# A hybrid decoder layer: attention's first q and k tiles, gate tiles and the evacuation of G put elsewhere in a planned order

## The chip, the cores and the metric

The kernel runs on one core of a Trainium2 chip. The metric is the time of one execution in microseconds (us), as the device measures it; the median of several runs counts. The engines are TensorE (PE), VectorE (DVE), ScalarE (ACT), GpSimd (POOL) and the DMA-issuing queue of SyncE (SP). Each runs its own instructions strictly in the order in which the program holds them.

## The reference

One layer over a sequence of 512 tokens, width 2048. The input is normalised and projected; half of the projection's columns feed 16 heads of dilated attention, half feed 16 heads of a recurrence (RWKV-7), and each half has a gate.

```python
h = rms_norm(x, norm_g[l])
proj = jnp.matmul(h, w_in[l]).astype(jnp.float32)
q, k, v, z_att, u_shift, z_rwkv = jnp.split(proj, splits, axis=-1)
att = dilated_mixture_attention(q, k, v, pos) * jax.nn.silu(z_att)
rwk = rwkv7_time_mix(u_shift, z_rwkv, ...)
x = x + jnp.matmul(jnp.concatenate([att, rwk], axis=-1), w_out[l])
return rms_norm(x, final_g)

# in dilated_mixture_attention: q, k rotated by position, three dilations
q = apply_rope(q.reshape(B, S, N_ATT_HEADS, HEAD_DIM), pos) * (HEAD_DIM ** -0.5)
k = apply_rope(k.reshape(B, S, N_ATT_HEADS, HEAD_DIM), pos)

# in rwkv7_time_mix, and one step of its recurrence
k = k * (1.0 + (a - 1.0) * k_a)
sa = jnp.einsum('bhij,bhj->bhi', state, a_t)
state = state * w_t + sa[..., None] * b_t + v_t[..., None] * k_t
y = jnp.einsum('bhij,bhj->bhi', state, r_t)
y = y_normed + bonus
return y * g * jax.nn.silu(z)
```

## The kernel before

**Tiles and fillers.** The projection is made in tiles of 128 columns for all 512 tokens. A tile takes 48 matmuls of 128x512: 16 slices of the contraction, three products each (weights and activations are split in a high and a low part, `whi`, `wlo`, `hh`, `hl`). The results are `mm_lora`, `mm_k`, `mm_r`, `mm_v` (the recurrence), `mm_z` (gates), `mm_gl`, `mm_qk` (attention's q and k); the attention's values come in three blocks `mv`. The weights arrive by SP's queue in tiles `raw_*` of 512 KB; ACT writes `whi` from them and DVE `wlo`. These matmuls are the fillers: they depend on little, and PE runs through them without a stop.

**The small work between them.** Python generators ("sides") hold the dependent steps: `pre`, `subst`, `build`, `scan`, `att`, `gate_g` and others. A side issues some instructions and then yields with an estimate and the tiles it needs next. After every filler matmul `step` calls `pump`, which lets go on those sides whose data a simple cost model of the engines holds to be ready. So the order of every engine's program is fixed when the kernel is built, and it is a guess: where a tile comes later than the model held, the in-order engine waits.

**The recurrent part** (to about 650 us). The 16 heads go as 8 pairs p, in chunks of 64 tokens. For each pair the tiles k, r, v are projected; `pre` makes the decay and rate (`pw`, `pa`, `wc`, `W`), the matrix `pM` of the triangular system and the bonus `pb`. `subst` solves the system in 62 steps that alternate between POOL's and DVE's tiles `XT`, `Xtmp`. Two merging steps follow (`zpb`), then `build`: two matmul groups `zf` whose results are copied to `L` by ACT and DVE, and four tiles G (`gp`, 128x512 each) which DVE multiplies by a mask into `X`. `scan` then runs over the chunks (`Y`, with `A`, `yc`), and `pF`, `pQ` prepare the next pair. Before all that `load_x` squares x, sums it into `acc`, and `rms` has PE sum `acc` over partitions (`pr`, `prb`); every projected result is scaled by `rstd` when it is evacuated, so the first evacuations (`first_evac`) wait for it.

**The attention** (650 to 965 us). 16 tiles `mm_qk`, four for each group g of four heads (two for q, two for k), are rotated (`rope_evac`, POOL and DVE, tiles `m`), and `assemble` moves the rotated rows by SP DMAs in pieces of 32 rows into `qa`, `ka`, from which ACT and DVE make high and low parts (`q`, `kd`, `kl`). `att` makes scores `s`, transposes `pt`, outputs `po` for each pair of heads. `att_consts` loads the rotary constants and masks into buffers `Lb`, `xt_b` of the recurrent part when that is done. Under the second half of the scores run the gate tiles z8 to z15 and, per pair, the recurrence's gate `pg`, whose weights `gw` are loaded by `gate_g`. The output projection (`raw_o`, `mo`, `mh`, `mt`) ends the program.

**What orders tiles** is the list at the program's end: `EARLY` says how many z tiles stand ahead of each pair's k, r, v, and `add_call` puts planner calls such as `until` between tiles.

Of the kernel before, what the change touches and what calls it, by code (L numbers as in the profile page):

```python
# [20 lines left out]
P = 128  # L21
# [115 lines left out]
def hymba_kernel(ctx: ExitStack, tc: tile.TileContext, xT, x, wa, wb, wo, pv, w2a2, g2, fg,  # L137
# [51 lines left out]
    bonesr = cp.tile([P, P], F32R, name="bonesr")  # L189
    hw0 = cp.tile([P, 16], F32, name="hw0")  # L190
    omu = cp.tile([P, 27], F32, name="omu")
    V.tensor_scalar(omu, pvt[:, 0:27], -1.0, 1.0, ALU.mult, ALU.add)
# [8 lines left out]
    def prologue():  # L201
# [7 lines left out]
        def squares():  # L209
            for k in range(KT):  # L210
                S.activation(xs[k], xs[k], AF.Square)
                if k == 1:
                    V.tensor_tensor(acc, xs[0], xs[1], ALU.add)
                elif k:
                    V.tensor_tensor(acc, acc, xs[k], ALU.add)
                if k % 2:
                    yield 0.0, S
            yield 2.0, acc
            yield from rms(acc)
# [34 lines left out]
    def later():  # L254
        bones = k2([P, P], "bones")
        Q.dma_start(bones, cst[:, 576:704])
        Q.dma_start(bmt, bmask)
        yield 1.59, bones
        V.tensor_copy(bonesr, bones)
        V.tensor_scalar(hw0, pvt[:, PV["w0"]:PV["w0"] + 16], 0.5, None, ALU.mult)  # L260
        for i in range(2):
            G.memset(xt_b[i], 0.0)
            G.tensor_copy(Lb[i][H[i], :, H[i]], ident[H[i], H[i]][:, None, :].to_broadcast([64, NCH, C]))
            yield 0.5, G
# [95 lines left out]
    def pump():  # L360
# [19 lines left out]
        mark[0] = model.clock  # L380

    def first_evac(f, a):
        while not normed:
            yield 0.675
        f(a)
        yield 0.6

# [53 lines left out]
    def run_main():  # L441
        for kind, name, fn in items:
            if kind == "c":
                fn()
            elif kind == "a":
                acc_ps = pm.tile([P, T], F32, tag="mm", name=f"mm_{name}")
                for kc in range(2):
                    hi, lo = feed.get()
                    for kk in range(8):
# [7 lines left out]
                        step()  # L457
                if normed:
                    after(2, lambda f=fn, a=acc_ps: f(a))
                else:  # L460
                    start(first_evac(fn, acc_ps))
# [156 lines left out]
    def pre(p, r, k, v):  # L618
# [82 lines left out]
        start(subst(p, Mp, rn2), 0.06, Mp, rn2, rank=-1)  # L701
        V.tensor_scalar(a, a, -1.0, col("k_a", p), ALU.add, ALU.mult)
        V.scalar_tensor_tensor(k, a, 1.0, k, ALU.add, ALU.mult)
# [109 lines left out]
    def build(p):  # L813
        while p not in state or p not in merged:
            yield 0.5
        st = state[p]
        X, L, FT, xt = (st[n] for n in ("X", "L", "FT", "xt"))
        for q in range(2):
            z = ps(f"zf{p}{q}", (P, 4, P))
            for c4 in range(4):  # L820
                for h in range(2):
                    TE.matmul(z[H[1 - h], c4, :], xt[H[h], 4 * q + c4, :], FT[H[h], 4 * q + c4, :], start=True, stop=True)
            for h in range(2):
                evac(L[h][H[1 - h], 4 * q:4 * q + 4, :], z[H[1 - h]])
            yield 0.3
        for q in range(2):
            for h in range(2):
                gp = ps(f"gp{p}{q}{h}", (P, 4, P))
                for c4 in range(4):
                    TE.matmul(gp[:, c4, :], L[h][:, 4 * q + c4, :], X[h][:, 4 * q + c4, :], start=True, stop=True)  # L830
                V.tensor_tensor(X[h][:, 4 * q:4 * q + 4, :], gp, gmask[h][:, None, :].to_broadcast([P, 4, P]), ALU.mult)
                yield 0.3
        built.add(p)
# [60 lines left out]
    rp, am = [], []  # L894

    def att_consts():
        for i in range(2):
            c_ = Lb[0].rearrange("p c t -> p (c t)")[:, i * T:(i + 1) * T]
            Q.dma_start(c_, rope[i])
            G.tensor_tensor(c_, c_, rstd, ALU.mult)  # L900
            rp.append(c_)
        for i, (o_, n_) in enumerate(((0, 384), (384, 384), (768, 512))):
# [14 lines left out]
    def v_evac(b, acc_ps):  # L917
# [7 lines left out]
        if b == 2:  # L925
            gtok = k1([P, 4, 32], "gtok")
            for t in range(4):
                S.activation(gtok[:, t, :], acc_ps[t][:, n:VB], AF.Copy, scale=rtok[:, t:t + 1])
            start(gl32(gtok), 1.023)

# [35 lines left out]

    pairs = {}

    def assemble(g, j, rot):
        raws = []  # L970
        for pr_ in range(2):
            for h in range(2):
                raw_ = k2([P, T], f"{'qk'[j]}a_{g}{pr_}{h}")
# [5 lines left out]
                raws.append(raw_)  # L979
            yield 5.1  # L980
        yield 0.225, *raws
        for pr_ in range(2):
            tl_ = pairs.setdefault(2 * g + pr_, {})
            if j == 0:
                q_ = k4([P, 2, T], f"q_{g}{pr_}", F32R)
                for h in range(2):
                    raw_ = raws[2 * pr_ + h]
                    S.activation(q_[:, h, :], raw_, AF.Copy)
                    r = H[1 - h]
                    V.tensor_tensor(q_[r, h, :], raw_[r], q_[r, h, :].bitcast(F32), ALU.subtract)  # L990
                tl_["q"] = q_
            else:
                for h in range(2):
                    raw_ = raws[2 * pr_ + h]
                    kd = k2([P, T], f"kd_{g}{pr_}{h}", F32R)
                    klo = k2([P, T], f"kl_{g}{pr_}{h}", F32R)
                    S.activation(kd, raw_, AF.Copy)
                    V.tensor_tensor(klo, raw_, kd.bitcast(F32), ALU.subtract)
                    tl_["k", h] = kd
                    tl_["kl", h] = klo  # L1000
            yield 2.874
        if j == 1:
            start(att(g))

# [4 lines left out]
    def att(g):  # L1009
        units = [(2 * g + pr_, t) for pr_ in range(2) for t in range(4)]  # L1010
        po, ssb_, pts = {}, {}, {}
        for u in range(len(units) + 2):
            if u < len(units):
                pair, t = units[u]
                tl_ = pairs[pair]
                n = max(256, 128 * (t + 1))
                nv = 128 * (t + 1)
                tsl = slice(t * P, (t + 1) * P)
                for h in range(2):
# [8 lines left out]
                    S.activation(ss[:, 0:nv], ss[:, 0:nv], AF.Exp, bias=nm, scale=-1.0, accum_out=den)  # L1028
                    ssb_[u, h] = (ss, den)
            if u >= 2:  # L1030
                pair, t = units[u - 2]
# [194 lines left out]
    add_aa((0, 9), ("lora", "k0"), (lora_evac, lambda a: rkv_evac(0, "k", 8, a)))  # L1226
    NZ, EARLY = 8, {2: 1, 3: 1, 4: 1, 5: 1, 6: 1, 7: 1}
    zs = iter(range(NZ))
# [7 lines left out]
    for p in range(NP):  # L1236
# [6 lines left out]
        add_a(1 + 16 + p, f"v{p}", lambda a, p=p: rkv_evac(p, "v", 16 + p, a))  # L1243
    add_z(NZ)
    add_a(41, "gl128", gl128_evac)
    add_call(lambda: until(lambda: NP - 1 in half))
    add_call(v_alloc)
# [5 lines left out]
    add_call(att_consts)  # L1253
    for g in range(4):
        for i in range(4):
            add_a(25 + 4 * g + i, f"qk{g}{i}", lambda a, g=g, i=i: rope_evac(g, i, a))
    for p in range(NP):
        add_call(lambda p=p: start(gate_g(p), 0.21))
        if p == NP - 1:
            add_call(lambda: pre_mix())  # L1260
        add_a(50 + p, f"z{8 + p}", lambda a, p=p: gate(8 + p, a))
    def pre_mix():
        drain()
# [128 lines left out]
```

## Time and profile before

| | |
|---|---|
| median of 3 runs | 1171.65 us (1171.32 to 1172.88) |
| profiled execution | 1172.79 us |
| its span in the trace | 1170.7 us |
| mean granted PE clock | 0.99 of 2.4 GHz |
| PE busy | 1133.5 us, 6878 instructions |
| DVE busy | 760.2 us |
| ACT busy | 544.0 us |
| POOL busy | 333.9 us |

The busy time of PE is a union of instructions that overlap; a filler of 128x512 lasts 0.39 us in the trace, and the next begins 0.23 us after it. Where PE is at the lower clock, or stands still, the table by stretches shows it. "Waited for" in the wait lists is the time that an engine stood idle before an instruction and the instruction that released it last.

### The profile page before, as it was taken

The numbers are of one execution on the slowest core, as the hardware profiler recorded it, in microseconds if no ns is written. First come the engines' busy times: TensorE is split into PE (matmuls) and PEld (weight loads), VectorE is DVE, ScalarE is ACT, GpSimd is POOL, SyncE is SP. The second block draws the span as 40 slices with busy tenths as digits, with TensorE's granted clock in tenths as the row PEclk, the third lists the DMA queues.
The fourth block names the chain that finished last, engine by engine and source line by source line (L and its number), as shares of the span: only waits on it lengthen the run. The fifth ranks groups of instructions, "written<-read, shape, count | busy, mean of one in ns | idle before, by whom it ended". The sixth has DMA issues, their size and how long they took to land. (4 is left out here: it accounts for less than half of the span.)

```text
span 1170.7 us, 19091 instructions
## 1 busy us (share of the span) xinstructions
PE 1133.5 (97%) x6878; PEld 943.2 (81%) x6878; DVE 760.2 (65%) x1521; ACT 544.0 (46%) x1209; POOL 333.9 (29%) x586
## 2 busy tenths in 40 slices
PE   7999999999999989999999999999999999999997
PEld 5777877788777878789999888888787877888897
DVE  6758867878887788787645555666666656243252
ACT  6444544655546464674533423455454444232233
POOL 1005882643865075644600121110000000011020
PEclk9999999999999989999999999999999999999999
DMA  7334342334242423333342545434344336444333
GB/s 263 101 92 127 105 128 73 95 104 117 78 123 89 115 83 95 91 97 105 88 109 77 162 128 154 123 118 140 109 139 138 117 118 211 126 126 132 103 127 144
DMA packets 89870, 139.62 MB, mean 119 GB/s; under 512 B 37936, under 2 KB 47664, under 8 KB 89776
## 3 DMA queue, kind: packets, MB, share of 16 engines
q1 hardware_dynamic: 89344, 137.83, 39.3%
q8 instruction: 54, 0.88, 0.3%
q10 hardware_dynamic: 432, 0.58, 0.1%
q14 instruction: 40, 0.33, 0.1%
HBM read 114.44 MB, written 14.75 MB: 110 GB/s over the span
## 5 line engine op out<-in xcount | busy, mean ns | idle before, releaser
L88 POOL TENSOR_TENSOR Xtmp<-XT,Mp 128x248 f32<-128x248 f32 (+30 forms) x248 | 128.9, 520 | 182.6 <-DVE XT L88 165.2
L88 POOL TENSOR_TENSOR XT<-XT,Xtmp 128x248 f32<-128x248 f32 (+30 forms) x248 | 142.2, 573 | 21.4 <-DVE XT L88 2.5
L88 DVE TENSOR_TENSOR wlo<-raw_o,whi 128x512 fp32r<-128x512 f32 x64 | 48.1, 792 | 87.5 <-ACT whi L88 87.5
L121 PE MATMUL mm_z<-hl,whi 128*128 128x512 f32 x256 | 103.3, 403 | 0.0
L121 PE MATMUL mm_z<-hh,wlo 128*128 128x512 f32 x256 | 103.0, 402 | 0.0
L121 PE MATMUL mm_z<-hh,whi 128*128 128x512 f32 x256 | 102.8, 402 | 0.0
L121 PE MATMUL mm_qk<-hh,whi 128*128 128x512 f32 x256 | 101.1, 395 | 0.8 <-ACT gtok L88 0.8
L121 PE MATMUL mm_qk<-hh,wlo 128*128 128x512 f32 x256 | 100.8, 394 | 0.0
L121 PE MATMUL mm_qk<-hl,whi 128*128 128x512 f32 x256 | 100.3, 392 | 0.0
L88 POOL TENSOR_TENSOR y<-y,fg 128x512 f32<-128x512 f32 (+1 forms) x16 | 19.3, 1240 | 254.7 <-ACT mo L88 235.9
L88 ACT ACTIVATE ss<-ss,nm 128x128 f32<-128x128 f32 (+3 forms) x64 | 35.5, 556 | 100.8 <-DVE nm L88 100.8
L88 ACT ACTIVATE whi<-raw_o 128x512 fp32r<-128x512 f32 x64 | 36.8, 623 | 95.5 <-PE mo L121 70.4
L88 POOL TENSOR_TENSOR m<-m,m 128x512 f32<-128x512 f32 x16 | 22.6, 1431 | 187.9 <-DVE m L88 144.8
L121 PE MATMUL mo<-whi,mh 128*128 128x512 f32 x192 | 74.7, 389 | 0.0
L121 PE MATMUL mo<-wlo,mh 128*128 128x512 f32 x192 | 74.7, 389 | 0.0
L121 PE MATMUL mo<-whi,ml 128*128 128x512 f32 x192 | 74.7, 389 | 0.0
L88 DVE TENSOR_TENSOR wlo<-raw_qk,whi 128x512 fp32r<-128x512 f32 x64 | 49.6, 795 | 33.1 <-ACT whi L88 29.0
L88 DVE TENSOR_TENSOR wlo<-raw_v,whi 128x352 fp32r<-128x352 f32 (+1 forms) x80 | 50.0, 655 | 26.9 <-ACT whi L88 26.4
L121 PE MATMUL mv<-whi,hh 128*128 128x352 f32 x192 | 63.6, 331 | 1.3 <-DVE vt L88 0.9
L121 PE MATMUL mv<-whi,hl 128*128 128x352 f32 x192 | 62.9, 328 | 0.0
L121 PE MATMUL mv<-wlo,hh 128*128 128x352 f32 x192 | 62.3, 325 | 0.0
L88 DVE TENSOR_TENSOR wlo<-raw_z,whi 128x512 fp32r<-128x512 f32 x64 | 47.9, 766 | 18.8 <-ACT whi L88 18.4
(300 smaller groups left out, 3016.7 us busy)
## 6 DMA issues: line engine op xcount, KB each, us to landing
raw_z<-in_wa_dram SPq DMA_DIRECT2D x32, 512.0 KB
raw_qk<-in_wa_dram SPq DMA_DIRECT2D x32, 512.0 KB
raw_o<-in_wo_dram SPq DMA_DIRECT2D x32, 512.0 KB
raw_v<-in_wb_dram SPq DMA_DIRECT2D x24, 352.0 KB
raw_r<-in_wa_dram SPq DMA_DIRECT2D x16, 512.0 KB
raw_v<-in_wa_dram SPq DMA_DIRECT2D x16, 512.0 KB
raw_k<-in_wa_dram SPq DMA_DIRECT2D x15, 512.0 KB
xk<-in_xT_dram SPq DMA_DIRECT2D x16, 256.0 KB
```

The lines of the kernel that those rows point to most:

```text
L88: return fn(o, *args, **kw)
L121: return fn(o, lhs, rhs, **kw)
```

## The change

- `pr`, the matmul that sums the squares, is asked for later (7.0 instead of 2.0 in the model's time), and first evacuations take turns.
- `(a - 1) k_a` moves from DVE to ACT, with a new constant `nka`.
- `build` waits for both copies of L before `gp`, and each G tile is evacuated in two halves, a copy on ACT and a masked multiply on DVE.
- The four q and k tiles of group 0 (`qk00` to `qk03`) stand ahead of the value blocks, and so do the rotary constants, now loaded to buffers of their own and multiplied on POOL there (`rope_consts`); `att_consts` copies them to `Lb`.
- `assemble` goes by pair of heads, waits for the last value block's evacuation and until the pair two before is scored, and `att` starts when the first pair's k is made.
- `gate_g` of a pair starts one gate tile earlier.
- `EARLY` puts all eight z tiles ahead of or among the pairs.

```diff
-            yield 2.0, acc
+            yield 7.0, acc
...
-        while not normed:
-            yield 0.675
+        turns.append(a)
+        return in_turn(f, a)
+
+    def in_turn(f, a):
+        while not normed or turns[0] is not a:
+            yield 0.3
         f(a)
+        turns.pop(0)
         yield 0.6
...
-        V.tensor_scalar(a, a, -1.0, col("k_a", p), ALU.add, ALU.mult)
+        S.activation(a, a, AF.Identity, bias=nka[:, p:p + 1], scale=col("k_a", p))
...
             yield 0.3
+        yield 0.1, L[0], L[1]
         for q in range(2):
             for h in range(2):
                 gp = ps(f"gp{p}{q}{h}", (P, 4, P))
+                o, qs = H[1 - h], slice(4 * q, 4 * q + 4)
                 for c4 in range(4):
                     TE.matmul(gp[:, c4, :], L[h][:, 4 * q + c4, :], X[h][:, 4 * q + c4, :], start=True, stop=True)
-                V.tensor_tensor(X[h][:, 4 * q:4 * q + 4, :], gp, gmask[h][:, None, :].to_broadcast([P, 4, P]), ALU.mult)
-                yield 0.3
+                S.copy(X[h][:, qs, H[h]], gp[:, :, H[h]])
+                V.tensor_tensor(X[h][:, qs, o], gp[:, :, o], gmask[h][:, None, o].to_broadcast([P, 4, C]), ALU.mult)
+                yield 0.1
...
+    def rope_consts():
+        for i in range(2):
+            c_ = k2([P, T], f"rope{i}")
+            Q.dma_start(c_, rope[i])
+            G.tensor_tensor(c_, c_, rstd, ALU.mult)
+            rp.append(c_)
+
     def att_consts():
         for i in range(2):
             c_ = Lb[0].rearrange("p c t -> p (c t)")[:, i * T:(i + 1) * T]
-            Q.dma_start(c_, rope[i])
-            G.tensor_tensor(c_, c_, rstd, ALU.mult)
-            rp.append(c_)
+            S.copy(c_, rp[i])
+            rp[i] = c_
...
     def assemble(g, j, rot):
-        raws = []
+        while not glt.get("v"):
+            yield 0.5
         for pr_ in range(2):
+            pair = 2 * g + pr_
+            while pair >= 2 and pair - 2 not in scored:
+                yield 0.5
+            raws = []
...
-    NZ, EARLY = 8, {2: 1, 3: 1, 4: 1, 5: 1, 6: 1, 7: 1}
+    NZ, EARLY = 8, {2: 1, 3: 1, 4: 2, 5: 1, 6: 1, 7: 2}
...
     add_a(41, "gl128", gl128_evac)
+    add_call(rope_consts)
+    add_qk(0)
...
-    for g in range(4):
-        for i in range(4):
-            add_a(25 + 4 * g + i, f"qk{g}{i}", lambda a, g=g, i=i: rope_evac(g, i, a))
+    for g in range(1, 4):
+        add_qk(g)
+    add_call(lambda: start(gate_g(0), 0.21))
     for p in range(NP):
-        add_call(lambda p=p: start(gate_g(p), 0.21))
-        if p == NP - 1:
+        if p < NP - 1:
+            add_call(lambda p=p: start(gate_g(p + 1), 0.21))
+        else:
             add_call(lambda: pre_mix())
```

On PE, in the first pair's tiles, `pr` stands in the r tile before:

```order
L121 MATMUL mm_r_385<-hl_169,whi_347 128x512
L121 MATMUL mm_r_385<-hh_168,wlo_348 128x512
L121 MATMUL mm_r_385<-hh_180,whi_347 128x512
L121 MATMUL pr<-ones,acc 128x1 x4
L121 MATMUL mm_r_385<-hl_181,whi_347 128x512
L121 MATMUL mm_r_385<-hh_180,wlo_348 128x512
```

And after, in the v tile:

```order
L121 MATMUL mm_v_458<-hh_107,whi_398 128x512
L121 MATMUL mm_v_458<-hl_108,whi_398 128x512
L121 MATMUL mm_v_458<-hh_107,wlo_399 128x512
L121 MATMUL pr<-ones,acc 128x1 x4
L121 MATMUL mm_v_458<-hh_119,whi_398 128x512
L121 MATMUL mm_v_458<-hl_120,whi_398 128x512
```

It moved back by 23 fillers: the 20 that are left of the r tile, and three of the v tile.

On PE, in the build of pair 4, the G matmuls stand right behind `zf` before (this is the place at 425 us of the trace):

```order
L121 MATMUL zf_4468<-FT_3868,xtf_232 64x128 x8
L121 MATMUL zf_4482<-FT_3868,xtf_232 64x128 x8
L121 MATMUL gp_4495<-X_4_3834,L_233 128x128 x4
L121 MATMUL gp_4501<-X_4_3835,L_236 128x128 x4
L121 MATMUL gp_4509<-X_4_3834,L_233 128x128 x4
L121 MATMUL gp_4515<-X_4_3835,L_236 128x128 x4
L121 MATMUL mm_k_4525<-hh_106,whi_4329 128x512
```

After:

```order
L121 MATMUL zf_4505<-FT_3854,xtf_233 64x128 x8
L121 MATMUL mm_z_4419<-hh_163,wlo_4311 128x512
L121 MATMUL mm_z_4419<-hh_169,whi_4354 128x512
L121 MATMUL mm_z_4419<-hl_170,whi_4354 128x512
L121 MATMUL mm_z_4419<-hh_169,wlo_4355 128x512
L121 MATMUL gp_4522<-X_4_3818,L_234 128x128 x4
L121 MATMUL mm_z_4419<-hh_181,whi_4354 128x512
L121 MATMUL gp_4530<-X_4_3819,L_237 128x128 x4
L121 MATMUL mm_z_4419<-hl_182,whi_4354 128x512
L121 MATMUL gp_4540<-X_4_3818,L_234 128x128 x4
```

Four fillers came between `zf` and `gp`, and one between two G tiles. On DVE the same tiles' second halves are these, with what each waits for:

```order
L88 COPY L_234<-zf_4493 64x512 [waits PE_49]
L88 COPY L_234<-zf_4505 64x512 [waits PE_49]
L88 TENSOR_TENSOR X_4_3818<-gp_4522,csts 128x4x64 [waits Activation_49]
L88 TENSOR_TENSOR X_4_3819<-gp_4530,csts 128x4x64 [waits Activation_49]
L88 TENSOR_TENSOR X_4_3818<-gp_4540,csts 128x4x64 [waits Activation_49]
```

Each DVE half waits for ACT, which copied the other half of the same tile.

On SP's queue, where the value blocks end, stood before:

```order
L133 DMA raw_qk_6918<-in_wa_dram 128x1024
L133 DMA L_233<-in_rope_dram 128x512 x2
L133 DMA L_236<-in_amask_dram 128x384 x2
L133 DMA xtf_232<-in_amask_dram 128x512
L133 DMA sp_y_6974<-yb_6913 128x512
L133 DMA raw_qk_6982<-in_wa_dram 128x1024
L133 DMA dup_6995<-d_gl_6965 32x512 x4
```

And after:

```order
L133 DMA raw_qk_7240<-in_wa_dram 128x1024
L133 DMA L_237<-in_amask_dram 128x384 x2
L133 DMA xtf_233<-in_amask_dram 128x512
L133 DMA qa_7270<-m_00_5640 32x512
L133 DMA qa_7270<-m_00_5803 32x512
```

The rotary constants are gone from here, and the pieces of the first pair's q (and then k, 16 in all) follow the masks.

## Rows read from the trace of the kernel before

**Rows 1.** The page: busy time, share of the span, instructions of each engine.
```profile
PE 1133.5 (97%) x6878; PEld 943.2 (81%) x6878; DVE 760.2 (65%) x1521; ACT 544.0 (46%) x1209; POOL 333.9 (29%) x586
```
**Rows 2.** PE's waits by what released them: us in total, times, longest.
```profile
PE gp L121 <- DVE L L88: 5.9, 3, 4.2
...
PE zpb L121 <- DVE xnb L88: 2.9, 3, 1.7
PE pr L121 <- DVE acc L88: 2.7, 1, 2.7
PE pM L121 <- DVE wc L88: 1.8, 1, 1.8
PE zpb L121 <- DVE zsb L88: 1.8, 1, 1.8
PE pg L121 <- ACT gh L88: 1.8, 1, 1.8
...
PE mm_qk L121 <- ACT gtok L88: 0.8, 1, 0.8
```
**Rows 3.** Stretches: length, PE, PEld, DVE, ACT, POOL busy; PEclk, DMA share, GB/s.
```profile
29.27:58.54 29.27, 26.58 (x112) 21.18 (x111) 21.15 (x49) 12.64 (x24) 0.35 (x2) 0.94 0.34 101
...
409.78:439.05 29.27, 24.46 (x149) 20.53 (x147) 23.82 (x37) 18.25 (x36) 21.74 (x36) 0.88 0.28 83
...
673.20:702.40 29.20, 29.20 (x131) 24.17 (x130) 16.45 (x20) 8.39 (x15) 5.98 (x4) 1.00 0.42 127
965.91:995.18 29.27, 26.90 (x110) 21.37 (x109) 19.09 (x32) 14.61 (x28) 0.00 (x0) 0.94 0.65 211
```
**Rows 4.** Timeline of PE at `pr`: start, length, instruction, idle time before it.
```profile
39.30 0.39 PE L121 MATMUL mm_r<-hh,wlo 128*128 128x512 f32 x1
39.53 0.39 PE L121 MATMUL mm_r<-hh,whi 128*128 128x512 f32 x1
42.61 1.05 PE L121 MATMUL pr<-ones,acc 128*128 128x1 f32 x8 [2.69 <-DVE acc L88]
```
**Rows 5.** Timeline of PE at `gp` of pairs 1 and 4.
```profile
224.83 1.16 PE L121 MATMUL gp<-X,L 128*128 128x128 f32 x8 [1.07 <-DVE L L88]
...
425.59 6.16 PE L121 MATMUL gp<-X,L 128*128 128x128 f32 x32 [4.21 <-DVE L L88]
```
**Rows 6.** Timeline of PE at the last `pg`.
```profile
971.39 0.50 PE L121 MATMUL pg<-g128h,gh 128*128 128x512 f32 x1 [1.75 <-ACT gh L88]
...
972.74 0.50 PE L121 MATMUL pg<-g128h,gl 128*128 128x512 f32 x1 [0.62 <-DVE gl L88]
...
973.66 0.63 PE L121 MATMUL mm_z<-hh,whi 128*128 128x512 f32 x1
```
**Rows 7.** Timeline of SP's queue, which issues the DMAs: start, length, tiles.
```profile
660.17 2.50 SPq L133 DMA_DIRECT2D dup<-d_gl  x4
...
679.65 4.95 SPq L133 DMA_DIRECT2D qa<-m  x8
...
960.13 5.28 SPq L133 DMA_DIRECT2D raw_o<-in_wo_dram  x2
965.46 2.29 SPq L133 DMA_DIRECT2D gw<-in_g_dram  x5
```
**Rows 8.** Instructions by form: count, busy us, mean ns, idle before, releasers.
```profile
L88 DVE TENSOR_TENSOR X<-gp,csts 128x512 f32<-128x512 f32 x32 | 21.7, 686 | 12.0 <-PE gp L121 11.7
L88 ACT COPY pa<-pt 128x256 f32<-128x256 f32 x48 | 16.7, 364 | 4.4 <-PE pt L121 4.4
...
L88 ACT ACTIVATE kd<-ka 128x512 fp32r<-128x512 f32 x16 | 9.3, 635 | 0.0
...
L88 DVE CUSTOM_DVE_ANT_0 ss<-s,L 128x256 f32<-128x256 f32 x16 | 6.1, 419 | 1.9 <-PE s L121 1.8
```
**Rows 9.** Timeline of ACT at the copy of the first `dup`.
```profile
664.84 0.63 ACT L88 ACTIVATE g32s<-dup 128x512 fp32r<-128x512 f32 x1 [4.88 <-DMA dup<-d_gl]
```
**Rows 10.** Timeline of POOL at the rotary constants.
```profile
655.89 3.00 POOL L88 TENSOR_TENSOR L<-L,rstd 128x512 f32<-128x512 f32 x2 [4.04 <-DMA L<-in_rope_dram]
```

More of the change, by code (lines that the diff above doesn't have):

```diff
@@ L190, in hymba_kernel @@
     hw0 = cp.tile([P, 16], F32, name="hw0")
+    nka = cp.tile([P, 8], F32, name="nka")
     omu = cp.tile([P, 27], F32, name="omu")
@@ L260, in later @@
         V.tensor_scalar(hw0, pvt[:, PV["w0"]:PV["w0"] + 16], 0.5, None, ALU.mult)
+        V.tensor_scalar(nka, pvt[:, PV["k_a"]:PV["k_a"] + 8], -1.0, None, ALU.mult)
         for i in range(2):
@@ L380, in pump @@
         mark[0] = model.clock
+    turns = []
     def first_evac(f, a):
-        while not normed:
-            yield 0.675
+        turns.append(a)
[3 more added lines that the diff above has]
+            yield 0.3
         f(a)
+        turns.pop(0)
         yield 0.6
@@ L457, in run_main @@
                         step()
-                if normed:
+                if normed and not turns:
                     after(2, lambda f=fn, a=acc_ps: f(a))
@@ L928, in v_evac @@
                 S.activation(gtok[:, t, :], acc_ps[t][:, n:VB], AF.Copy, scale=rtok[:, t:t + 1])
+            glt["v"] = True
             start(gl32(gtok), 1.023)
@@ L965, in rope_evac @@
             start(assemble(g, j, (m[0], m[2])), 0.1, m[0], m[2])
-    pairs = {}
+    pairs, scored, ready = {}, set(), set()
     def assemble(g, j, rot):
-        raws = []
+        while not glt.get("v"):
+            yield 0.5
         for pr_ in range(2):
+            pair = 2 * g + pr_
+            while pair >= 2 and pair - 2 not in scored:
+                yield 0.5
+            raws = []
             for h in range(2):
@@ L979, in assemble @@
                 raws.append(raw_)
[L980 to L983, printed above, removed]
+            yield 0.225, *raws
+            tl_ = pairs.setdefault(pair, {})
             if j == 0:
@@ L986, in assemble @@
                 for h in range(2):
-                    raw_ = raws[2 * pr_ + h]
-                    S.activation(q_[:, h, :], raw_, AF.Copy)
+                    S.activation(q_[:, h, :], raws[h], AF.Copy)
                     r = H[1 - h]
-                    V.tensor_tensor(q_[r, h, :], raw_[r], q_[r, h, :].bitcast(F32), ALU.subtract)
+                    V.tensor_tensor(q_[r, h, :], raws[h][r], q_[r, h, :].bitcast(F32), ALU.subtract)
                 tl_["q"] = q_
@@ L993, in assemble @@
                 for h in range(2):
-                    raw_ = raws[2 * pr_ + h]
                     kd = k2([P, T], f"kd_{g}{pr_}{h}", F32R)
                     klo = k2([P, T], f"kl_{g}{pr_}{h}", F32R)
-                    S.activation(kd, raw_, AF.Copy)
-                    V.tensor_tensor(klo, raw_, kd.bitcast(F32), ALU.subtract)
+                    S.activation(kd, raws[h], AF.Copy)
+                    V.tensor_tensor(klo, raws[h], kd.bitcast(F32), ALU.subtract)
                     tl_["k", h] = kd
                     tl_["kl", h] = klo
-            yield 2.874
-        if j == 1:
-            start(att(g))
+                ready.add(pair)
+                if pr_ == 0:
+                    start(att(g))
+            yield 1.0
     def two(pa, t):
@@ L1014, in att @@
                 pair, t = units[u]
+                while pair not in ready or (t == 0 and u == 0 and pair >= 2 and pair - 1 not in scored):
+                    yield 0.5
                 tl_ = pairs[pair]
@@ L1029, in att @@
                     ssb_[u, h] = (ss, den)
+                if t == 3:
+                    scored.add(pair)
             if u >= 2:
@@ L1244, in hymba_kernel, with add_qk @@
     add_z(NZ)
+    def add_qk(g):
+        for i in range(4):
+            add_a(25 + 4 * g + i, f"qk{g}{i}", lambda a, g=g, i=i: rope_evac(g, i, a))
     add_a(41, "gl128", gl128_evac)
+    add_call(rope_consts)
+    add_qk(0)
     add_call(lambda: until(lambda: NP - 1 in half))
```

## The prediction

> **What bounds the kernel now.** I read the engines' totals first [rows 1]: PE is busy 97% of the span and DVE 65%. Time can come off only where PE stands still or runs slowly, so the next views were PE's waits grouped by what released them, and then a table by stretches of 29.27 us with the granted clock beside the busy time. The waits [rows 2] are short and scattered: 5.9 us of `gp` for the tile L (4.2 of them in one place), 2.9 and 1.8 of `zpb`, 2.7 of `pr`, 1.8 of the first `pM`, 1.8 of the last `pg`. Nearly all end with a DVE or ACT instruction. The table [rows 3] shows a second loss in the same places. Where PE waits nothing, as at 673 us, it is busy 29.20 of 29.20 us at clock 1.00. In the slices with `pr` and with the last `pg` the mean clock is 0.94, and in the one with the long `gp` wait 0.88. Two more slices, around `zpb` waits at 350 and 477 us, read like the `pr` one. A mean of 0.94 is the lower level, 1.2 instead of 2.4 GHz, for a few us: 0.06 x 29.27 = 1.8 us, of which I count 1.6, since PE was not busy all of it. So a wait of about 2 us costs about 3.5. The whole that can be won is some 27 us of waits (with the small ones) and about 9 us of clock. DVE, busy 23.82 of 29.27 us in the slice at 410 us (81%), is the engine nearest to becoming a bound in the recurrent part.
>
> **The change part by part.** The amount of PE work is the same before and after (5117 rows of order in both); what changes is where the small matmuls stand.
>
> *The norm's sum, `pr`.* In the trace `pr` comes 42.61 us into the span and waits 2.69 us for `acc` [rows 4]. It moves 23 fillers down the order; at the 0.23 us from one filler to the next in the same rows that is 5.3 us, twice the wait, so it goes: -2.7, and -1.6 for the clock. What it pushes is the chain behind it. Only 6 fillers now stand between `prb` and the first `mm_k` that needs a new accumulator bank (30 before), and the banks are freed by evacuations that need the norm. No row shows a wait there. It lies between 0 and the 2.7 us removed; I take 0.7, because 24 fillers fewer are 5.5 us less cover for a chain that starts 5.3 - 2.7 = 2.6 us later on the clock. Net -3.6 (range -4.3 to -1.6). The `pM` of head pair 0 waits 1.8 for `wc` [rows 2]; it now stands later in v1, and I leave it 0.3: -1.5.
>
> *The G matmuls, `gp`.* At 425.59 us all sixteen stand in a row directly behind `zf`, and PE waits 4.21 us for the copies of L [rows 5]. After the change four fillers (0.9 us) stand between, in every pair, and no place without fillers is left. The two copies of L end the wait; they sit behind other DVE work, so I leave 1.0 of the 5.9 us: -4.9. In the long wait the clock fell: 32 records of `gp` took 6.16 us where 8 at full clock take 1.16 [rows 5]. Four times 1.16 is 4.6, so at least 1.5 us is lost, and more since the 1.16 holds a drain that counts once: -2.0.
>
> Each G tile was evacuated by one DVE multiply of 0.686 us; now ACT copies one half and DVE multiplies the other. The nearest rows are a copy of 128x256 on ACT, 0.364, and a DVE instruction of that size, 0.419 [rows 8]. The order puts a wait on ACT at each DVE half, so the two run one after the other: 0.78 us and a handover instead of 0.69. DVE is relieved by 0.27 x 32 = 8.5 us and of eight multiplies in `pre`, and ACT takes them. The `Y` that needs the last G tile has 3 fillers as cover instead of 4 or 5: a loss of 0 to 0.3 us in each of 8 pairs, I take 1.2 in all. PE's order has 26 more changes from one tile to another. The first matmul after a change lasts 0.50 instead of 0.39 us [rows 4, 6], so this is 0 to 2.9; I take 0.8, which leaves 2.0 with the other.
>
> The page "PSUM — Partial Sum Buffer" of the Trainium skill, in its section on bank collisions, says that two engines must not touch one bank in the same 32 partitions at a time. The two halves of a G tile lie in one bank and all partitions, so by the page they can't overlap, which is what the order's wait says; no run here shows an overlap. Overlapped, the chain would be 0.42 instead of 0.78 and the term near -1 instead of +1.2.
>
> *The last gate, `pg`.* It waits 1.75 us at 971.39 for `gh`, then again for `gl` (0.6 us, the next record), and the filler behind it lasts 0.63 instead of 0.39 us [rows 4, 6]. Its load `gw` was issued at 965.46, behind two loads of the output projection that held SP's queue for 5.28 us [rows 7]. The gate now starts one tile earlier and `gw` stands ahead of `raw_o`: -2.4 and -1.6, together -4.0.
>
> *The other waits of the recurrent part.* `zpb` lost 2.9 + 1.8 us, and two clock falls (3.2) went with it: 7.9 us. The fillers between `pM` and the last `zpb` group (the cover of the substitution on POOL and DVE) were 241 to 278 and are 273 to 300. The places that waited had 241 and 247, and 26 more are 5.9 us. That speaks for all of it going; DVE at 81% [rows 3] speaks for some to come back elsewhere. I take half, -4.0, with -8 (all gone) and +5 (two new ones with their clock) as bounds.
>
> *Rotary constants on POOL.* They are loaded and multiplied amid the substitution of pair 6, after 44 of its 62 steps. Before they cost 3.0 us of POOL behind 4.04 us of waiting for the load [rows 10]. The chain is delayed by 7.0 us, more if SP's queue is late. Its cover is 291 fillers, 44 more than the 247 that lacked 1.8 us: 10.0 - 1.8 = 8.2 us of margin. I take +1.0 (0 to 4).
>
> *First scores.* Before, the q and k of the first heads had 104 fillers after k's rotation; now their tiles lie far ahead, but their assembly starts with the attention constants, about when the value blocks end. From there SP issues three masks and 16 pieces. Eight pieces take 4.95 us [rows 7], so 9.9, and 1.4 for the masks. The landing is nearest to that of `dup`: four issues from 660.17 to 662.67, and ACT's copy of it at 664.84, 2.2 us behind [rows 7, 9]. Then `kd` on ACT, 0.635 [rows 8], and `kl` on DVE, much the same: 14.8 us. On PE 41 fillers and a `pg` stand ahead of the scores, 41 x 0.23 + 0.9 = 10.3, the first filler waits 0.8 for `gtok` as before [rows 2], and SP is some 0.8 ahead of PE: 14.8 - 0.8 - 11.1 = 2.9 us of wait (1.5 to 4), and half of a clock fall, +0.8. Together +3.7. The scores of later groups have 72 fillers after the last k tile (16.5 us) against 4.95 + 2.2 + 1.3 us and the rotation: no wait counted.
>
> *The rest*: z tiles moved into pairs 4 and 7 change no work (cost nothing if their weights come as the others do; a wait of one raw load otherwise); `first_evac` in turn is in the 0.7 above.
>
> **Sum**: -3.6 - 1.5 - 4.9 - 2.0 + 2.0 - 4.0 - 4.0 + 1.0 + 3.7 = -13.3 us. The profiled run took 1172.79 us, span 1170.7; that is 1.1 above the median 1171.65. Against the median: 1158.
>
> **The rivals.** *A, the stalls move.* Nearly every wait in rows 2 ends with DVE, which is 81% busy there; fillers put ahead of one consumer are taken from another, and G's new halves chain DVE to ACT. Then the terms of `gp` and of the other waits (-10.9) come back somewhere else and -2.4 is left: 1169. For it: the list is scattered, so no single producer is late. Against: 8.5 us and eight multiplies leave DVE.
>
> *B, slower: the assembly by pair comes too late for the scores.* One SP queue carries the loads of weights and the pieces. A weight load waits for its buffer, and everything behind it waits too. If the pieces of pairs 0, 2 and 4 each stand behind such a load, one more tile half, 5.4 us (24 fillers), is added to the 2.9 and a clock fall of 1.6: 9.9 us in three places, 29.7 instead of 3.7, so +12.7: 1184. It decides from 17.0 / 3 = 5.7 us a place. For it: now a pair waits until an earlier pair is scored, and nothing is made ahead. Against: 72 fillers of cover at pairs 2 and 4.
>
> *C, the rotary loads are late.* They stand on SP behind the pair's other transfers and a weight load. If POOL stands 16 us, 8 lie outside the margin, with a clock fall +9.5 instead of +1: 1167.
>
> *D, the two-engine evacuation doesn't split the time*: it is already counted as serial, and moves nothing more than the 1.2.
>
> **How the numbers follow.** The forecast (1150 to 1166 by its bounds) 0.62, A 0.17, C 0.08, B 0.13. A difference under 0.2% (2.3 us) can't be told from none. Faster than 1169.3: the forecast, C, and half of A, 0.78; slower: B, 0.13; within: 0.09. The range reaches down to 1148, where all recurrent waits go and the first scores wait 1.5, and up to 1171, which takes in C and A.
>
> **What would show it.** In the changed profile: no `pr<-acc` and no `gp<-L` over 1 us in PE's waits; the slices at 30, 410 and 966 us back to a clock near 1.00; one wait of about 3 us at the first `s`, with `kl` or `kd` as releaser; POOL waiting for the rotary load in the middle of pair 6. `zpb` waits of over 3 us in qk02 would show C, `s` waits at three places B, and a recurrent part in which the sum of PE's waits is as before, A. If the z tiles moved forward or the order on ACT (which takes over two jobs) made PE wait, I was wrong about what is free.

## The result, and the profile after

| | changed kernel | kernel before, beside it |
|---|---|---|
| median | 1182.44 us (1180.32 to 1185.02) | 1171.62 us |
| ratio to before | 1.0091 (95%: 1.007 to 1.0113) | |
| span of the profiled run | 1182.6 us | 1170.7 us |

The change makes the kernel 10.8 us slower. Forecast was 1158, with a range from 1148 to 1171; the sign was wrong, and the time lies outside the range.

The totals of the page, against [rows 1]:

```profile
PE 1149.7 (97%) x6878; PEld 941.8 (80%) x6878; DVE 742.1 (63%) x1522; ACT 560.8 (47%) x1243; POOL 334.1 (28%) x586
```

PE has the same 6878 instructions and is busy 16 us longer. DVE lost 18 us of work and ACT gained 17, as work was moved from one to the other. PE's waits, against [rows 2] (us in total, times, longest):

```profile
PE s L121 <- DVE kl L88: 6.4, 3, 3.5
...
PE zpb L121 <- DVE xnb L88: 1.8, 2, 1.2
...
PE s L121 <- ACT kd L88: 1.3, 1, 1.3
...
PE mv L121 <- DVE m L88: 1.1, 1, 1.1
PE pM L121 <- DVE bt L88: 1.0, 1, 1.0
```

The rows for `gp`, `pr`, and the last `pg` are gone. What is new is the scores `s`, 7.7 us in four waits. The stretches, against [rows 3] (length, PE, PEld, DVE, ACT, POOL busy, granted clock, DMA share, GB/s):

```profile
29.27:58.54 29.27, 29.27 (x130) 23.45 (x129) 20.60 (x49) 12.92 (x25) 0.11 (x2) 1.00 0.38 120
409.78:439.05 29.27, 28.80 (x236) 22.84 (x235) 20.92 (x39) 15.17 (x33) 16.93 (x27) 1.00 0.37 114
...
761.02:790.29 29.27, 26.69 (x120) 20.44 (x120) 16.61 (x43) 11.34 (x29) 2.56 (x2) 0.94 0.39 111
965.91:995.18 29.27, 29.27 (x132) 23.48 (x128) 17.12 (x28) 9.81 (x19) 0.00 (x0) 1.00 0.60 193
```

The three slices in which the clock had been low are at 1.00, with PE almost full. So the waits of `pr`, of `gp` and of the last `pg` did go, and still the kernel is slower. One place shows both reasons. Timeline of PE (start, length, instruction, idle time before it) at the first scores of pair 2:

```profile
769.18 0.40 PE L121 MATMUL mm_qk<-hh,whi 128*128 128x512 f32 x1
769.41 0.40 PE L121 MATMUL mm_qk<-hl,whi 128*128 128x512 f32 x1
769.64 0.40 PE L121 MATMUL mm_qk<-hh,wlo 128*128 128x512 f32 x1
769.88 0.40 PE L121 MATMUL mm_qk<-hh,whi 128*128 128x512 f32 x1
770.11 0.40 PE L121 MATMUL mm_qk<-hl,whi 128*128 128x512 f32 x1
770.35 0.39 PE L121 MATMUL mm_qk<-hh,wlo 128*128 128x512 f32 x1
770.58 0.28 PE L121 MATMUL s<-kd,q 128*128 128x256 f32 x1
773.34 0.39 PE L121 MATMUL s<-kl,q 128*128 128x256 f32 x1 [2.48 <-DVE kl L88]
```

First, a filler follows the other by 1.17 / 5 = 0.234 us, where it was 0.227 before (the medians of all such steps of `mm_qk` say the same). This distance from one start to the next is called the pitch below. Its growth is not the wait, and not the granted clock either, which falls only behind the wait, at 774.8 us, and gives the stretch its mean of 0.94. It holds in the whole program, also in the output projection, whose order the change doesn't touch. Two rows show it, PE alone in the stretch from 1010 to 1070 us (length, busy time, instructions, clock, DMA share, GB/s), of the kernel before and of the changed one:

```profile
1010.00:1070.00 60.00, 60.00 (x266) 1.00 0.38 114
```

```profile
1010.00:1070.00 60.00, 60.00 (x259) 1.00 0.38 114
```

In 60 us without any wait PE has 266 matmuls before and 259 after (one or two of them were begun ahead of the stretch). Over all 575 steps of `mo` the mean pitch is 226.67 ns before and 233.32 ns after, 6.7 ns more.

Second, PE waits for `kl` of pair 2. DVE's and SP's timelines show why:

```profile
768.15 0.69 DVE L88 TENSOR_TENSOR yl<-yl,po 128x512 f32<-128x512 f32 x1 [6.50 <-DMA yl<-sp_s]
768.76 1.28 DVE L88 TENSOR_TENSOR m<-mm_qk,L 128x512 f32<-128x512 f32 x2
770.07 1.40 DVE L88 TENSOR_TENSOR q<-qa,q 64x512 fp32r<-64x512 f32 x2
771.40 1.28 DVE L88 TENSOR_TENSOR wlo<-raw_qk,whi 128x512 fp32r<-128x512 f32 x2
772.61 1.28 DVE L88 TENSOR_TENSOR kl<-ka,kd 128x512 fp32r<-128x512 f32 x2
```

```profile
755.12 4.95 SPq L133 DMA_DIRECT2D qa<-m  x8
760.18 4.96 SPq L133 DMA_DIRECT2D ka<-m  x8
765.18 0.58 SPq L133 DMA_DIRECT2D yl<-sp_s  x1
```

DVE stands for 6.50 us in front of the multiply by `yl`, a gate tile that was spilled and is fetched back. SP issues that load at 765.18, behind the 16 pieces of the pair. Everything on DVE behind the multiply, `kl` as the last, comes later by that.

### The profile page after: what moved, and what is told of

Read it like the earlier page. It is cut to its first block, busy times and chain, and to the rows that moved or that the text cites. A ratio compares the mean times of both kernels' runs of the same rounds, so it can differ in the third digit from the quotient of the medians.

```text
span 1182.6 us, 19112 instructions
## 1 busy us (share of the span) xinstructions
PE 1149.7 (97%) x6878; PEld 941.8 (80%) x6878; DVE 742.1 (63%) x1522; ACT 560.8 (47%) x1243; POOL 334.1 (28%) x586
## 5 line engine op out<-in xcount | busy, mean ns | idle before, releaser
L88 POOL TENSOR_TENSOR Xtmp<-XT,Mp 128x248 f32<-128x248 f32 (+30 forms) x248 | 132.4, 534 | 168.5 <-DVE XT L88 151.1
L88 POOL TENSOR_TENSOR XT<-XT,Xtmp 128x248 f32<-128x248 f32 (+30 forms) x248 | 139.3, 562 | 21.7 <-DVE XT L88 2.1
L121 PE MATMUL mm_qk<-hh,whi 128*128 128x512 f32 x256 | 104.8, 410 | 0.8 <-ACT gtok L88 0.8
L121 PE MATMUL mm_qk<-hl,whi 128*128 128x512 f32 x256 | 104.2, 407 | 0.0
L121 PE MATMUL mm_qk<-hh,wlo 128*128 128x512 f32 x256 | 104.1, 407 | 0.0
L88 DVE TENSOR_TENSOR wlo<-raw_qk,whi 128x512 fp32r<-128x512 f32 x64 | 45.0, 716 | 31.8 <-ACT whi L88 31.7
L88 ACT ACTIVATE whi<-raw_v 128x352 fp32r<-128x352 f32 (+1 forms) x80 | 41.3, 543 | 38.8 <-PE mv L121 25.8
```

Source lines behind the costliest of these rows:

```text
L88: return fn(o, *args, **kw)
L121: return fn(o, lhs, rhs, **kw)
```

## The experiments

Medians in us; "before" is the kernel before, run beside it on the same chip. The intervals are of the ratio to it. The last column is the number of instructions in the row shown above for the stretch from 1010 to 1070 us: 266 is the pace of the kernel before, 259 that of the changed one.

| run | median | before | ratio (95%) | matmuls in 1010 to 1070 us |
|---|---|---|---|---|
| changed kernel | 1182.44 | 1171.62 | 1.0091 (1.007 to 1.0113) | 259 |
| e1, nka 32 columns | 1182.11 | 1173.18 | 1.0076 (1.006 to 1.0093) | 259 |
| e2, nka 16 columns | 1179.64 | 1173.18 | 1.0059 (1.004 to 1.0078) | 264 |
| e3, before, 32 bytes more | 1180.86 | 1173.18 | 1.0068 (1.0051 to 1.0084) | 259 |
| e4, before, hh by 32, rest by 64 | 1180.69 | 1173.18 | 1.0068 (1.0049 to 1.0086) | 259 |
| e5, nka behind all | 1171.45 | 1173.59 | 0.9985 (0.9973 to 0.9997) | 267 |
| e7, before, 256 bytes more | 1172.98 | 1173.59 | 0.9997 (0.9987 to 1.0007) | 266 |
| e8, before, all by 32 | 1173.32 | 1173.59 | 1.0002 (0.9987 to 1.0017) | 266 |
| e9, e5 and yl fetched early | 1165.54 | 1173.85 | 0.9934 (0.9918 to 0.995) | |
| e10, e9 and scores later | 1161.37 | 1173.85 | 0.9891 (0.9874 to 0.9907) | |
| e11, e9, G by DVE alone | 1174.0 | 1173.85 | 1.0005 (0.9993 to 1.0017) | |
| e12, e9, pr early again | 1171.09 | 1173.85 | 0.9982 (0.9969 to 0.9996) | |
| e13, before, weights alone by 32 | 1182.35 | 1172.01 | 1.0085 (1.0066 to 1.0105) | 258 |

**Why every filler is slower.** The change leaves the output projection's matmuls and their order as they were; what it can change there is where tiles lie. Tiles and pools lie one behind the other in each partition, and the new constant `nka`, 8 columns of float32, takes 32 bytes in the second pool. All that is allocated behind it, the weight tiles `whi` and `wlo` too, moved 32 bytes; the activations `hh`, `hl` and, in their place, `mh`, `ml` lie in the first pool and stayed.

```diff
-    nka = cp.tile([P, 8], F32, name="nka")
+    nka = cp.tile([P, 32], F32, name="nka")[:, 0:8]      # e1; e2: [P, 16]
```

> The changed kernel with one edit: the constant nka is 32 columns wide instead of 8 (128 bytes of a partition instead of 32; 8 columns are used), so every tile that is allocated behind it lies 96 bytes further on and the weight tiles whi, wlo start at a multiple of 128 bytes again, as before the change. The order of all engines is that of the changed kernel. Address theory: the pitch of a 128x512 filler, 233.3 ns in the changed kernel, goes back to 226.7 ns; some 3360 fillers x 6.67 ns = 22.4 us come off 1182.4, so about 1160 us, 1 per cent faster than before. Rival (the new order itself makes PE slower, by contention or by its clock): pitch stays at 233 ns and the time at 1182 us.

> The changed kernel with nka 16 columns wide (64 bytes): whi and wlo start at an odd multiple of 64 bytes. If a 64-byte boundary is enough, the pitch is 226.7 ns and the time as in the run with 32 columns, about 1160 us; if 128 bytes are needed, 233.3 ns and 1182 us. Rival (order): 1182 us.

```diff
     hw0 = cp.tile([P, 16], F32, name="hw0")
+    spare = cp.tile([P, 8], F32, name="spare")           # e3
+    nc.vector.memset(spare, 0.0)
```

> The kernel before with one unused tile of 8 columns (32 bytes), filled once with zeros, at the place where the change puts nka; nothing else. Address theory: pitch 233.3 instead of 226.7 ns, 22 us slower, about 1194 us. Rival (order): no change, 1171.6 us.

```diff
+    sph = hp.tile([P, 8], F32, name="sph")               # e4: ahead of hh, with e3's tile
+    nc.vector.memset(sph, 0.0)
     pvt = cp.tile([P, NPV], F32, name="pvt")
```

> The kernel before with two unused tiles of 8 columns, one ahead of the activations hh, hl (and mh, ml, which take their place), one at nka's place: hh, hl, mh, ml are shifted by 32 bytes and all else, whi and wlo too, by 64. In the projection hh is the moving operand and whi the stationary one, in the output projection whi moves and mh is stationary. If any operand off a 64-byte boundary costs the 6.67 ns, both kinds of filler are at 233 ns: about 1194 us. If it is the weight tiles alone, all at 227 ns: 1172 us. If it is the moving operand alone, mm at 233 and mo at 227 (and in the run before this one the other way round, which the changed kernel's trace, with both at 233, speaks against).

e3 settles half of it: the kernel before with 32 unused bytes and no other edit has the 259 matmuls of the changed kernel (233.3 ns), and is 7.7 us slower. But e1, with `whi` on a 128-byte boundary as before the change, is as slow as the changed kernel, 259 matmuls, and the theory of a boundary fell. e2 lies between: 228.9 ns in the output projection, though `mm_qk` had a median of 234. What fits all four is the distance of the weight tiles from the activations. In the kernel before, by the sizes of the tiles between them, it is a multiple of 512 bytes. It became 32 bytes more in the changed kernel, in e3 and in e4 (64 less 32), 128 in e1, 64 in e2. Three runs test that.

```diff
-    nka = cp.tile([P, 8], F32, name="nka")
...
     sp = ctx.enter_context(tc.tile_pool(name="sp", bufs=4))
+    nka = sp.tile([P, 8], F32, tag="nka", bufs=1, name="nka")   # e5: the last pool
```

> The changed kernel with the constant nka (8 columns) taken from the pool that is allocated last instead of from the constants' pool, so that hh, hl, mh, ml, whi, wlo and all large buffers lie exactly where they lay before the change; the order of all engines is that of the changed kernel. Distance theory, formed after the four runs before this one (a 128x512 filler is at its best only where the distance of whi from hh in a partition is a multiple of 512 bytes, as it is in the kernel before): filler pitch 226.7 ns in the output projection (233.3 in the changed kernel), and the time falls from 1182 to about 1162 to 1168 us, below the kernel before. Rival (any new program is slower, whatever its addresses): pitch 229 to 233 ns and 1180 us.

```diff
+    sph = hp.tile([P, 8], F32, name="sph")               # e8: ahead of hh
+    nc.vector.memset(sph, 0.0)
     pvt = cp.tile([P, NPV], F32, name="pvt")
```

> The kernel before with one unused tile of 8 columns ahead of hh, so that hh, hl, whi, wlo and everything else are shifted by the same 32 bytes. Distance theory: pitch 226.7 ns and no change from before (1172 to 1174 us). If what counts is where a tile starts (32 bytes off), pitch 233 ns and 1181 us, as in the run in which whi alone was shifted.

```diff
     hw0 = cp.tile([P, 16], F32, name="hw0")
+    spare = cp.tile([P, 64], F32, name="spare")          # e7
+    nc.vector.memset(spare[:, 0:8], 0.0)
```

> The kernel before with an unused tile of 64 columns (256 bytes) at nka's place: whi and wlo 256 bytes further from hh. Distance theory with 512 bytes: pitch above 226.7 ns, somewhere between 229 and 233, and about 1177 to 1181 us. If a multiple of 256 bytes is enough: 226.7 ns and 1172 to 1174 us.

All three went the way of the distance. e8 shifts both sides by 32 bytes, so that each tile lies off every larger boundary: 266 matmuls, no change in time. e7 shows that 256 bytes are enough: 226.67 ns again. In e5 PE's order is that of the changed kernel to the last instruction, and only the place of one constant differs. PE's row for it:

```profile
1010.00:1070.00 60.00, 60.00 (x267) 1.00 0.37 115
```

Against before it went from +10.8 us to -2.1 us, so the place of `nka` cost 12.9 us here. The last run shifts the weight tiles alone (`raw`, `whi`, `wlo` by 32 bytes; the second spare tile makes the shift of all later pools 256 bytes, which cost nothing in e7):

```diff
+    spw = wp.tile([P, 8], F32, tag="spw", bufs=1, name="spw")   # e13
+    nc.vector.memset(spw, 0.0)
+    spk = kp.tile([P, 56], F32, tag="spk", bufs=1, name="spk")
+    nc.vector.memset(spk[:, 0:8], 0.0)
     pvt = cp.tile([P, NPV], F32, name="pvt")
```

> The kernel before with an unused tile of 8 columns (32 bytes) at the start of the pool that holds the weight tiles raw, whi and wlo, and one of 56 columns (224 bytes) at the start of the next pool, so that raw, whi, wlo alone lie 32 bytes further on; the constants, L, xtf and the activations lie where they lay, all later buffers 256 bytes further, which cost nothing in the run with 256 bytes. Distance theory: the fillers, which read whi or wlo and hh, hl, mh or ml, go to a pitch of 233.3 ns, and the time to about 1181 us, as in the run with everything behind nka's place shifted. Rival (the shifted constants, L or recurrent buffers are what costs): 226.7 ns and 1173 us.

```profile
1010.00:1070.00 60.00, 60.00 (x258) 1.00 0.38 116
```

It is 10.3 us slower than before, with 233.3 ns, so it is these tiles and not the constants or the recurrence's buffers. Why the distance matters stays open: one may guess that PE's reads of its two operands meet in the memory, but no run shows the memory. The value blocks `mv` (128x352) keep a median of 160 ns at every distance that was run.

The loss (7.7 us in e3, 10.3 in e13, 12.9 for `nka`) is less than 3360 fillers x 6.7 ns = 22 us. Two numbers of e3 account for much of that. The mean of `mm_qk` went from 231.2 to 236.1 ns, not by 6.7, as some of its steps are that slow or late before too. And from 26 us to the end of the value blocks PE's waits of over 0.15 us shrank from 19.0 us in all to 14.2: slower fillers give the small work more cover.

**Why the scores wait.** With the distance put right, e5 still gains only 2 us (0.4 to 3.2 by the interval) where 13 were forecast. Its spans before and after the start of the attention tell where: the last value-block matmul ends at 680.53 us, and 192 fillers more than before lie ahead of it, 43.5 us at 226.7 ns. Without them that is 637.0, against 651.52 before: 14.5 us won up to there. At the end of the span 2.9 are left. PE's waits in e5:

```profile
PE s L121 <- DVE kl L88: 7.1, 4, 3.6
...
PE s L121 <- ACT kd L88: 1.3, 1, 1.3
```

These 8.4 us, and four falls of the clock with 1.7 us each (at 694 and 766 us, and a double one at 827), are 15.2; the last `pg` gave 4 back. In e9, which is e5 with one more edit, the fetch of the spilled tile is moved two steps ahead:

```diff
-                elif t == 2 and f"s{pair}" in spill:
+                elif t == 0 and f"s{pair}" in spill:
                     fetch_y(pair, f"s{pair}")
```

> The run with nka behind all (1171.45 us), and one edit more: a pair's spilled gate tile yl is fetched when its first transposed scores are made (t == 0), not its third (t == 2), so that on SP this load stands ahead of the 16 pieces of the next group and not behind them. In the run before, PE waited 2.83 us at 761 us and 3.57 us at 825 us for kl of pairs 2 and 4, and DVE stood 6.7 and 7.4 us in front of the multiply by yl, which is queued ahead of kl. Theory (DVE's queue held by that load): those two waits shrink to under 1 us each and the clock falls at 766 and 827 us go with them; 9 to 11 us come off, 1161 to 1163 us. Rival (the pieces themselves land late, or a weight load holds SP): waits and time stay, 1171 us.

DVE and SP of e9 at the same place:

```profile
755.80 0.69 DVE L88 TENSOR_TENSOR yl<-yl,po 128x512 f32<-128x512 f32 x1 [2.65 <-PE po L121]
756.66 1.29 DVE L88 TENSOR_TENSOR m<-mm_qk,L 128x512 f32<-128x512 f32 x2 [0.17 <-PE mm_qk L121]
757.98 1.41 DVE L88 TENSOR_TENSOR q<-qa,q 64x512 fp32r<-64x512 f32 x2
759.31 1.28 DVE L88 TENSOR_TENSOR kl<-ka,kd 128x512 fp32r<-128x512 f32 x2
```

```profile
738.02 0.45 SPq L133 DMA_DIRECT2D yl<-sp_s  x1
...
746.78 4.96 SPq L133 DMA_DIRECT2D qa<-m  x8
751.84 4.96 SPq L133 DMA_DIRECT2D ka<-m  x8
```

DVE now waits for PE and not for the load, and `kl` is done before the scores ask. PE's waits for `s` in e9:

```profile
PE s L121 <- ACT kd L88: 2.9, 3, 1.3
PE zpb L121 <- DVE zsb L88: 2.4, 3, 1.3
PE s L121 <- DVE kl L88: 2.3, 4, 1.0
PE zpb L121 <- DVE xnb L88: 2.0, 2, 1.2
```

The two waits of 2.8 and 3.6 us for `kl` are gone, and the kernel is 5.9 us faster. It was less than the 9 to 11 expected: the planner, with an earlier fetch, also put the scores earlier in the order, by 7 fillers for pair 2, 30 for pair 4 and 33 for pair 6, and those of pairs 4 and 6 now wait 1.2 and 2.0 us, the second with a clock fall. The theory stands, the size was off.

```diff
                     yield 0.5
+                if u == 0:
+                    yield 2.8 if pair == 0 else 1.8      # e10, on e9
                 tl_ = pairs[pair]
```

> The run with the early fetch, and the first scores of every group asked for later in the planner's time (2.8 us for pair 0, 1.8 us for the others), which puts 13 fillers more ahead of the scores of pair 0 and 8 more ahead of those of pair 2. The wait of 2.0 us at the first scores and its clock fall (1.6 us) should go: 1157 to 1160 us, 3 us less than without the delay. Rival (the delay pushes later stages and they wait instead): as without it or slower.

PE's first waits in e10:

```profile
PE mm_lora L121 <- ACT whi L88: 5.7, 2, 5.3
PE zpb L121 <- DVE zsb L88: 2.7, 3, 1.3
PE pt L121 <- DVE den L88: 2.6, 2, 2.0
```

No `s` is among the waits, and no clock fall is left between 28 us and the tail. Some of the rival came: the transpositions `pt` behind the delayed scores wait 2.0, 0.6 and 0.9 us. The net is 4.2 us less than e9. e10 is the fastest of all: 12.5 us below the kernel before.

**Single parts of the change.** Both on e9.

```diff
-                o, qs = H[1 - h], slice(4 * q, 4 * q + 4)
+                qs = slice(4 * q, 4 * q + 4)
...
-                S.copy(X[h][:, qs, H[h]], gp[:, :, H[h]])
-                V.tensor_tensor(X[h][:, qs, o], gp[:, :, o], gmask[h][:, None, o].to_broadcast([P, 4, C]), ALU.mult)
-                yield 0.1
+                V.tensor_tensor(X[h][:, qs, :], gp, gmask[h][:, None, :].to_broadcast([P, 4, P]), ALU.mult)
+                yield 0.3
```

> The run with the early fetch, with G evacuated by one DVE multiply again (ACT's half copies gone, the wait for both L kept). If the serial halves cost what the prediction put in its sum (1.2 us in all, at the Y behind the last G tile), this is 0 to 2 us faster than the early-fetch run. If the relief of DVE (8.5 us of busy time) is worth more than that, it is slower, by 1 to 4 us, with waits for DVE tiles in the recurrent part.

```profile
PE zpb L121 <- DVE xnb L88: 7.7, 3, 3.4
...
PE zpb L121 <- DVE zsb L88: 2.8, 2, 2.2
```

8.5 us slower than e9. `zpb`, which ends the substitution on DVE and POOL, waits 10.5 us where e9 has 4.4, with two clock falls (213 and 421 us) that e9 doesn't have, although more fillers stand between `pM` and the first `zpb` here (its cover: 285 to 338, against 274 to 300 in e9); e9's fall at 695 us is missing here. DVE is busy 752.0 us against 742.3. So the split of G seems to pay by what it takes off DVE's queue, and not at G itself. That is argued: the undoing also let the planner place other work, and no run separates the two.

```diff
-            yield 7.0, acc
+            yield 2.0, acc
```

> The run with the early fetch, with the norm's sum asked for at 2.0 again instead of 7.0, so that pr stands 22 fillers earlier, as in the kernel before. By the prediction's step this brings back the 2.7 us wait for acc near 40 us and the clock fall behind it and removes a wait of about 0.7 at the first bank: 3.6 us slower than the early-fetch run (1.6 to 4.3). Rival (the later pr only pushes the wait to the first evacuations): no difference.

```profile
PE pF L121 <- DVE L L88: 2.1, 2, 1.9
...
PE pF L121 <- ACT L L88: 1.6, 1, 1.6
PE pr L121 <- DVE acc L88: 1.4, 1, 1.4
```

5.6 us slower, above the 1.6 to 4.3 of the step, and by another way. `pr` itself waits 1.4 us with no clock fall; the larger part is in the first pair's `pF` at 103 to 107 us, 3.5 us of waiting, and behind it 6.8 us at the lower clock, which cost half of that.

## Why the prediction was wrong

*The recurrent part* was forecast at -13.0 us (all terms up to the rotary constants: -3.6 - 1.5 - 4.9 - 2.0 + 2.0 - 4.0 + 1.0) and measured at -14.5 in e5, with the tiles in place. The waits named for `pr`, `gp` and the `pM` of pair 0 went, and the clock reads 1.00 in these slices, so the mechanism held there. That the sum came out so near is in part luck. Of the -13.0, some -7.8 are waits and -5.2 the clock. In e5 the waits of over 0.15 us from 26 us to the end of the value blocks are 11.5 us against 19.0, so -7.5, but not place by place: `gp` and `pr` gave all, while `zpb`, of whose 4.7 us half was to go, still waits 4.3, and `pM` and `pb` wait 3.4 where they waited 2.4. The clock gave more, four falls of 17.1 us in all, at half speed 8.5 us (the one behind `gp` was 6.8 us long and cost 3.4, not 2.0).

The cover that was to explain `zpb` doesn't sort its waits. Counted from `pM` to the first `zpb` in the trace of before, pairs 0, 3 and 5 have 278, 263 and 241 fillers and wait 0.9, 1.8 and 1.8 us; pair 2 has 245 and doesn't wait. The reading of 241 and 247 for the two places at 350 and 477 us is right for the second only.

The 2.0 us for G's serial halves and for the changes of tile didn't show as waits (`Y` waits 0.8 us for DVE once), and by e11 the split may be a gain, through the relief of DVE, which the prediction had named and given no term.

*The last gate*, -4.0: its wait and its clock fall are gone.

*The first scores*, +3.7: 2.9 us of wait and half a clock fall were forecast; in e5 pair 0 waits 0.3 + 1.3 + 0.4 = 2.0, with a whole fall of 1.7. Right, and within the 1.5 to 4.

*Rotary constants*, +1.0: POOL's timeline in the changed kernel has them in the middle of pair 6's substitution:

```profile
524.02 2.74 POOL L88 TENSOR_TENSOR rope<-rope,rstd 128x512 f32<-128x512 f32 x2 [10.49 <-DVE d_gl L88]
```

The row names a DVE tile, but SP issued the load at 518.69 us only, and in e5, with PE and POOL in the same order, the row names the load:

```profile
516.14 2.77 POOL L88 TENSOR_TENSOR rope<-rope,rstd 128x512 f32<-128x512 f32 x2 [10.15 <-DMA rope<-in_rope_dram]
```

So it was most likely the load that was late, as rival C had it, but by less than C's 16 us. The chain was delayed by 10.5 + 2.7 = 13.2 us, more than the 7.0 taken and more than the margin of 8.2, and yet `zpb` of that pair waits only 0.6 us. The term is within its 0 to 4, but the margin behind it was not right; why it was larger stays open.

*Rival D*, the serial evacuation, was right in form:

```profile
L88 DVE TENSOR_TENSOR X<-gp,csts 128x256 f32<-128x256 f32 x32 | 13.2, 422 | 20.2 <-ACT X L88 20.2
L88 ACT COPY X<-gp 128x256 f32<-128x256 f32 x32 | 11.5, 370 | 14.9 <-PE gp L121 14.8
```

All of DVE's waiting ends with ACT's copy, and the durations are close to those of [rows 8] (419 and 364 ns). No DVE half starts before ACT's has ended (31 ns or more behind it, in all 32). That agrees with the Trainium skill's page "PSUM — Partial Sum Buffer", section on bank collisions, by which two engines must not be in one bank in the same 32 partitions at a time. PE has no wait at `gp` in the changed kernel.

The prediction failed in two steps.

**"what changes is where the small matmuls stand"** left out an edit of one line. `nka` and its 32 bytes had no term. They made each 128x512 filler 6.7 ns longer in the whole program, 12.9 us in all (the changed kernel's +10.8 against e5's -2.1). It was a cost put at nothing. No rival had it, and the trace of before couldn't show it, as the weight tiles there lie at a distance that costs nothing.

**"The scores of later groups have 72 fillers [...] no wait counted"** followed the pieces from SP to `kd` and `kl`, and not what is queued on DVE ahead of `kl`. That queue holds the multiply by `yl`, and `yl`'s load stands behind the pieces on SP. It cost 2.8 and 3.6 us of wait and three clock falls of about 1.7, some 11.5 us by the trace of e5. Rival B had named these two places and a price of 9.9 each, but with the wrong cause, a load of weights. That its 1184 lies near the measured 1182 is chance: 12.9 us of the result come from the pitch, which B doesn't have.

The sum: from the forecast of -13.3 to e5's -2.1 are 11.2 us, which is about what the scores cost, and from there to the +10.8 of the result 12.9, the distance. e10, with the tiles in place, the fetch early and the scores later, stands at -12.5 against its kernel before. It also delays the first scores, which the forecast had left at +3.7, so it is not the forecast kernel itself.

## What to carry to other kernels

A new tile is an edit to all tiles allocated behind it. Before costing a change, list what it allocates ahead of the matmuls' operands, keep small constants behind the large buffers, and compare the pitch of a stretch of untouched matmuls in both traces first: it tells in one row whether the whole program has changed its pace. Where transfers are moved ahead on one queue, follow the load that they are moved past to its consumer, and see what stands behind that consumer on its engine.

## What the hardware showed unexpectedly

The pitch of a 128x512 float32 matmul with a new stationary operand each time depends on the distance between the two operands' places in a partition. The distance is counted from the place of the activations to that of the weights. In the output projection: 226.67 ns where it is a multiple of 256 bytes (before, e5, e7, e8), 233.3 ns at 32 or 128 more (the changed kernel, e1, e3, e4, e13), 228.9 ns at 64 more (e2). In `mm_qk`, where the activations move and the weights are stationary, the medians are 227 ns at a multiple of 256, 232 at 128 more (e1), and 234 or 233 at 64 and at 32 more, so the two kinds of filler do not lose alike. Other distances weren't run. In the stretch from 1010 to 1070 us the granted clock reads 1.00 in all of them, and PE reads as 100% busy, so neither busy share nor clock gives it away.

The clock also fell after two short waits in a row: in e9 at 879.6 us, behind waits of 0.98 and 1.02 us that ended at 876.7 and 878.1, and in the changed kernel at 703.1 us, behind 1.30 and 0.40 that ended at 702.0 and 702.8. The length of a single wait doesn't sort them: a wait of 1.75 us at 477 us had a fall behind it in the trace of before, one of 1.97 us at 707 us in e10 had none. Nor do the same waits bring the same falls each time: with PE's order as in the kernel before, e8 waited 2.3 us for `pr` and had no fall there.
